# A two-block transformer kernel on one core: first loads, norms at layer boundaries, and the order of gates and compression in the second block

## The chip, the core and the metric

The kernel runs on one core of one Trainium2 chip. The metric is the device time of one execution in microseconds (us); lower is better. A core has a matrix engine (TensorE, PE in the profile; its weight loads are PEld), VectorE (DVE), ScalarE (ACT), GpSimd (POOL) and SyncE (SP), which here only issues DMAs. Each engine works through its own instructions in order. Operands lie in SBUF, matrix products land in PSUM (eight banks of 128 x 512 float32).

## What is computed

`reference()` runs two blocks, one behind the other, in float32. Cut to what matters:

```python
def first_block(x, c, ctx, c_ctx, ...):        # x: 256 tokens x 1024, ctx: 256 tokens x 1024
    for l in range(2):
        sh1, sc1, g1, sh2, sc2, g2 = adaln(c, w_mod[l], b_mod[l])     # silu(c) @ w_mod + b_mod, six rows of 1024
        h  = modulate(rms_norm(x, norm1_g[l]), sh1, sc1)              # rms_norm(x) * g * (1 + sc) + sh
        q, k, v, u_pool, a_conv, b_conv = project_inputs(h, w_in[l], ...)
        ... # differential attention over ctx and x, pooling, convolution of a * sigmoid(b)
        x = x + g1 * (mix @ w_out[l])
        x = x + g2 * swiglu(modulate(rms_norm(x, norm2_g[l]), sh2, sc2), w_ffn_in[l], w_ffn_out[l])
        # in layer 0 the same for ctx, with c_ctx; layer 1 leaves ctx as it is
    return x

def hybrid_layer(x, ...):                      # second block
    z = rms_norm_2(x) @ w_in                   # twenty parts
    y_a = forgetting attention with cumsum(log_sigmoid(f))            # "fox"
    y_b = rg_lru(conv(xb)): a = exp(-8 r softplus(-lam)), gates r, i = sigmoid(...)
    y_c = nsa_attention: keys and values compressed by silu(t @ w1) @ w2, then chosen and windowed
    y_d = gelu(u) * spatial gating of gelu(v)
    merged = sum_n sigmoid(mg_n) * ((y_n * silu(gate_n)) @ w_branch_n)
    return x + merged @ w_out
```

## The kernel before

Activations are kept with features on partitions: `xT` is 128 x 8 x 512, eight tiles `k` of 128 features; columns 0 to 255 are the context, 256 to 511 the input. Weights stream from memory in chunks of 128 x 1024 float32 (512 KB). `weights()` (L339) loads one into `wraw` (4 buffers), ScalarE rounds it to float32r (`whi`, 3 buffers), VectorE forms the rest (`wlo`, 3 buffers). Every large product is then three matmuls, `mm3` (L353): hi x hi, hi x lo, lo x hi. Activations are split alike into `hH` and `hL`.

Order. The code is traced in program order; a planner with a simulated timeline then chooses the order on each engine, by readiness and program order. `tc.issue_after(i)` binds that order: what is traced inside is queued behind `i` on the engine of `i`, and on that engine alone; it is an order of issue, not a wait. All weight loads go out on SP's queue.

Stages, and the names that the change touches:

- **First stage.** `xT` is loaded by two DMAs on ScalarE's queue (L298). Squares, `rows_of_rstd` (L470): the reciprocal norm, 16 matmuls with one column (L432), a power on GpSimd (L359), and a product with ones that spreads it over partitions (L447). `modulation(l, group)` (L502) multiplies silu(c) with eight chunks of `w_mod`, four column groups of 32 at a time (L508), copies, transposes (L515) and adds the bias. Shift and scale come in two halves of eight chunks (`MOD_GROUPS`, first two entries); the chunks use `wraw` and `wmod` (2 buffers) in turn. `norm` (L478) makes per k and per half of the tokens: one VectorE product (L490), the ScalarE part with the shift (L492) and the VectorE rest (L493). Then the four tiles of convolution inputs (`ab`), 24 matmuls of 512 columns each: `feats` (L370) runs the first three of them, with the modulation and norm of the second half between their halves.
- **Layer 0 and 1.** `layer_scalars` (L592), attention, then `project_rows` (L864): the last three of eight output rows are done first for one half of the tokens and then for the other, so that the norm of the first half can begin. `after` (L982) starts the norm for the feed-forward part as soon as the last row is there, `after2` (L1018) that of the next layer. `feats` then runs the first products.
- **Second block.** Token products (`toks`), `log_sigmoid` for 16 and for 4 columns (L1217), the compression: 32 float32 products of 128 x 128 weights with 32 columns (L1146), NSA attention with gate products (`jobs`) between the heads, `batch` (L1455) of activations, the fox attention with `lru_gates` (L1343) traced behind its first head, and the branch products.

## Time and profile before

| | before |
|---|---|
| median of 3 runs | 1428.55 us (1427.3 to 1432.38) |
| the profiled execution, its own time | 1427.89 us |
| span of its instructions | 1426.1 us, 1.8 us lie around it |
| PE busy | 1350.7 us (95%) |
| DVE, ACT, POOL busy | 965.0, 615.3, 237.4 us |
| moved from memory | 210.98 MB, 149 GB/s over the span |
| mean granted PE clock | 0.965 of 2.4 GHz |

PE's clock has two levels here, 2.4 and 1.2 GHz; a stretch with a granted clock of 0.59 spent most of its time on the lower. Idle time of an engine counts only where the end of the kernel waits for it, so the stretches in which PE stands or runs at the lower level are what to look at.

### The profile page before, as it was taken

What the parts mean: (1) busy time and instruction counts of PE and PEld (TensorE: products, weight loads), DVE (VectorE), ACT (ScalarE), POOL (GpSimd) and SP (SyncE); (2) the same over time, 40 slices, a digit from 0 to 9 for tenths busy, and PEclk for the clock granted to TensorE, in tenths of its full rate; (3) what the DMA queues carried; (4) which work ended last, traced back from release to release, by engine and by line L of the source; (5) the groups of instructions that cost most, each with busy time, mean ns of one, the idle gap of its engine ahead of it and who ended that gap; (6) DMA issues with size and microseconds to landing.
All of it is one profiled execution on the core that took longest, in us unless ns stands there. A gap on an engine that the chain in (4) does not pass through costs nothing. (4 is left out here: it accounts for less than half of the span.)

```text
span 1426.1 us, 22731 instructions
## 1 busy us (share of the span) xinstructions
PE 1350.7 (95%) x8750; PEld 1185.2 (83%) x8750; DVE 965.0 (68%) x1924; ACT 615.3 (43%) x1094; POOL 237.4 (17%) x274
## 2 busy tenths in 40 slices
PE   4999999899999999999988899999989998999999
PEld 2699657788888888888966899999877887988999
DVE  4599666677766677738966655555776666657565
ACT  3334454433222222235355443444634558546443
POOL 0056530410000000014534300000442002000000
PEclk8999999899999999999989899999988999999999
DMA  8423541335445567623301355554733423434553
GB/s 327 181 88 134 172 153 45 134 121 190 160 148 166 192 219 238 209 85 104 119 30 60 119 170 185 171 196 159 243 127 111 141 94 105 134 106 158 181 187 125
DMA packets 61309, 213.52 MB, mean 150 GB/s; under 512 B 6928, under 2 KB 8080, under 8 KB 60944
## 3 DMA queue, kind: packets, MB, share of 16 engines
q1 hardware_dynamic: 60768, 209.90, 43.8%
q10 hardware_dynamic: 432, 2.16, 0.4%
q8 instruction: 69, 1.13, 0.3%
q14 instruction: 40, 0.33, 0.1%
HBM read 210.98 MB, written 1.05 MB: 149 GB/s over the span
## 5 line engine op out<-in xcount | busy, mean ns | idle before, releaser
L344 ACT CAST whi<-wraw 128x1024 fp32r<-128x1024 f32 (+2 forms) x296 | 304.8, 1033 | 534.4 <-PE ps_mm L355 243.4
L345 DVE TENSOR_TENSOR wlo<-wraw,whi 128x1024 fp32r<-128x1024 f32 (+2 forms) x296 | 359.3, 1216 | 173.8 <-ACT whi L344 171.5
L354 PE MATMUL ps_mm<-hH,whi 128*128 128x256 f32 (+1 forms) x1056 | 345.1, 329 | 11.1 <-ACT hH L492 9.0
L355 PE MATMUL ps_mm<-hL,whi 128*128 128x256 f32 (+1 forms) x1056 | 342.3, 325 | 1.7 <-DVE hL L493 1.7
L356 PE MATMUL ps_mm<-hH,wlo 128*128 128x256 f32 (+1 forms) x1056 | 342.0, 325 | 0.9 <-DVE wlo L345 0.8
L354 PEld LDWEIGHTS ps_mm<-hH,whi 128*128 128x128 f32 x1056 | 204.3, 195 | 32.8 <-ACT hH L492 11.1
L355 PEld LDWEIGHTS ps_mm<-hL,whi 128*128 128x128 f32 x1056 | 204.4, 194 | 18.8 <-DVE hL L493 3.1
L356 PEld LDWEIGHTS ps_mm<-hH,wlo 128*128 128x128 f32 x1056 | 204.2, 194 | 17.1 <-DVE wlo L345 2.0
L354 PE MATMUL ps_mm<-hidH,whi 128*128 128x256 f32 (+1 forms) x683 | 214.8, 317 | 3.0 <-ACT hidH L350 1.7
L355 PE MATMUL ps_mm<-hidL,whi 128*128 128x256 f32 (+1 forms) x683 | 215.2, 316 | 0.6 <-DVE hidL L351 0.6
L356 PE MATMUL ps_mm<-hidH,wlo 128*128 128x256 f32 (+1 forms) x683 | 214.4, 316 | 0.0
L355 PE MATMUL ps_mm<-wlo,hH 128*128 128x256 f32 (+2 forms) x464 | 145.5, 315 | 4.1 <-DVE wlo L345 4.0
L356 PE MATMUL ps_mm<-whi,hL 128*128 128x256 f32 (+2 forms) x464 | 143.3, 311 | 0.0
L354 PE MATMUL ps_mm<-whi,hH 128*128 128x256 f32 (+2 forms) x464 | 141.3, 313 | 2.0 <-ACT tm L642 1.5
L354 PEld LDWEIGHTS ps_mm<-hidH,whi 128*128 128x128 f32 x683 | 129.5, 190 | 12.0 <-ACT hidH L350 1.9
L355 PEld LDWEIGHTS ps_mm<-hidL,whi 128*128 128x128 f32 x683 | 129.6, 190 | 9.5 <-DVE hidL L351 1.2
L356 PEld LDWEIGHTS ps_mm<-hidH,wlo 128*128 128x128 f32 x683 | 129.5, 190 | 8.1
L465 POOL TENSOR_TENSOR squares<-squares,scr 128x256 f32<-128x256 f32 (+1 forms) x28 | 31.6, 1127 | 561.5 <-ACT scr L464 561.0
L575 DVE CUSTOM_DVE_ANT_0 ps_md<-wmod,tm 128x512 f32<-128x512 f32 x160 | 111.5, 697 | 10.8 <-DMA wmod<-in_w_dram 7.9
L359 POOL TENSOR_TENSOR st<-st,mhalf 128x4 f32<-128x4 f32 (+3 forms) x54 | 69.1, 1284 | 201.7 <-DVE st L627 88.6
L843 DVE SCALAR_TENSOR_TENSOR xT<-ps_mm,modv,xT 128x256 f32<-128x256 f32 x116 | 52.5, 479 | 73.4 <-PE ps_mm L356 73.4
L355 PEld LDWEIGHTS ps_mm<-wlo,hH 128*128 128x128 f32 x464 | 89.5, 193 | 11.4 <-DVE wlo L345 7.1
(345 smaller groups left out, 2011.6 us busy)
## 6 DMA issues: line engine op xcount, KB each, us to landing
wraw<-in_w_dram SPq DMA_DIRECT2D x271, 512.0 KB, 3.4
wmod<-in_w_dram SPq DMA_DIRECT2D x85, 512.0 KB, 4.2
wraw<-in_w_dram SPq DMA_DIRECT2D x32, 448.0 KB, 3.2
xT<-in_x_dram ACTq DMA_DIRECT2D x2, 1024.0 KB, 6.9
single<-in_w_dram SPq DMA_DIRECT2D x8, 256.0 KB, 7.6
wraw<-in_w_dram SPq DMA_DIRECT2D x4, 288.0 KB, 3.5
tm<-in_rows_dram SPq DMA_DIRECT2D x4, 256.0 KB, 6.5
out_dram<-scr SPq DMA_DIRECT2D x8, 128.0 KB, 1.7
```

The lines of the kernel that those rows point to most:

```text
L344: act.copy(out=hi[:, :m], in_=t[:, :m])
L345: P["split"] = dve.tensor_tensor(lo[:, :m], t[:, :m], hi[:, :m].bitcast(F32), op=ALU.subtract)
L354: pe.matmul(ps, a[0], b[0], start=start, stop=False)
L355: pe.matmul(ps, a[0], b[1], start=False, stop=False)
L356: P["product"] = pe.matmul(ps, a[1], b[0], start=False, stop=stop)
L359: pool.tensor_tensor(t, t, mhalf[:, :n], op=ALU.pow)
L465: eng.tensor_tensor(squares[:, lo:hi], squares[:, lo:hi], q, op=ALU.add)
L575: dve.tensor_tensor_reduce(bank("md"), t[:, i * 512:i * 512 + 512], crow[2 * j + i], 1.0, 0.0, ALU.mult, ALU.add, sums[j][:, i * KD + d:i ...
L843: dve.scalar_tensor_tensor(xT[:, d, r], ps[:, s * 256 - lo:s * 256 - lo + 256], M(l, which, 1 - s)[:, d:d + 1], xT[:, d, r], op0=ALU.mult, ...
```

## The change

- The input is loaded by four DMAs on SP's queue, ahead of the weights. Scale and shift come in four quarters of two tiles k each (`first_modulation`, chunks with both); the `ab` weights are packed by the same quarters, for all four tiles at once (`abq`). The sixteen modulation chunks use nine `hid` buffers (now 128 x 1024, hi and lo halves of one tile) and the two `wmod`. `first_products` goes quarter by quarter.
- `weights()` can be queued behind given instructions (`P["behind"]`), and with `P["both"]` every second rounding is done by VectorE (from NSA head 6 to fox head 2).
- `project_rows` holds back six rows instead of three for the attention output of layer 0, and takes a `mm` bank for each half row. In layer 0 the norm of the input half is queued behind the first product of the feed-forward part; at the end of layer 0 that of the context behind the first product of layer 1.
- In layer 1 the first three products of the feed-forward part use `xT * scale` without the norm; the result is multiplied by the norm afterwards, and the shift's share comes from one-column float32 products (24 in all).
- `layer_scalars` is queued behind the norm and the first products; the constants' loads behind the last modulation load.
- `log_sigmoid` for 4 columns moves into the feed-forward part of layer 1, that for 16 columns behind the compressed scores. The compression is turned round: `tbs` (32 columns) is the weight, `w1` streams 128 columns, four column groups; a copy and a product with `sum4` add the groups.
- `batch` chains its activations one behind the other, and behind the last exponentials of NSA; `gb` goes before `gd`; `lru_gates` follows at once, its four Tanh ahead of its four Exp.

```diff
+        if l == 0:
+            for q in range(4):
+                cols = np.arange(q * 256, q * 256 + 256)
+                for k in range(0, 8, 2):
+                    rows(("first", q, k), "w_mod", (l,), np.concatenate([D + cols, cols]), k * 128, 2)
+                rows(("abq", q), "w_in", (l,), np.arange(1792, 2304), q * 256, 2)
-    for k in range(0, KD, 4):
-        act.dma_start(out=xT[:, k:k + 4], ...)
+    for k in range(0, KD, 2):
+        dma.dma_start(out=xT[:, k:k + 2], ...)
     def weights(key):
+        behind = P.pop("behind", ())
...
-        act.copy(out=hi[:, :m], in_=t[:, :m])
+            P["count"] += 1
+            if P["both"] and P["count"] % 2:
+                dve.tensor_copy(hi[:, :m], t[:, :m])
+            else:
+                act.copy(out=hi[:, :m], in_=t[:, :m])
+    def first_modulation(q, pools, p):
+        ps = bank(p)
+        for k in range(0, KD, 2):
+            t = raw_chunk(("first", q, k), next(pools))[0]
+            P["first"] = P["load"]
+            for i in range(2):
+                for g in range(4):
+                    o = i * 512 + g * 128
+                    pe.matmul(ps[g * 32:g * 32 + 32, :128], csil[:, k + i, :], t[:, o:o + 128],
+                              start=(k + i == 0), stop=(k + i == KD - 1), tile_position=(0, g * 32))
+            yield
+        cp = P["wk"].tile([128, 256], F32, name="cp")[:, :128]
+        act.copy(out=cp, in_=ps[:, :128])
+        pe.transpose(ps[:, 256:384], cp, ident)
...
+    def first_products(items):
+        pools = iter(("hid",) * 9 + ("wmod",) * 2 + ("hid",) * 5)
+        ps = [bank("mm" if i < 3 else "sc") for i in range(4)]
+        mods = [first_modulation(q, pools, ("md", "sc")[q % 2]) for q in range(4)]
+        for q in range(4):
+            if q:
+                P["behind"] = P["normed"], P["rest"]
+            wH, wL = weights(("abq", q))
+            for _ in mods[q]:
+                pass
+            norm(h, 0, 512, parts(0, 0, scale1, (0, 1)), range(2 * q, 2 * q + 2), row, True)
+            for k in range(2):
+                for (key, _), t in zip(items, ps):
+                    c = slice(key[2] * 128, key[2] * 128 + 128)
+                    mm3(t, (wH[:, k, c], wL[:, k, c]), tuple(x[:, 2 * q + k] for x in h), q + k == 0, q + k == 4)
+                if q < 3:
+                    with tc.issue_after(P["product"].ins):
+                        next(mods[q + 1])
+                        next(mods[q + 1])
+        P["behind"] = P["normed"], P["rest"], P["first"]
...
-        late = d_list[-3:] if lo == 0 and final else ()
+        late = d_list[-(6 if which == 2 else 3):] if lo == 0 and final else ()
...
+        def unnormed_feat(key, evac):
+            wH, wL = weights(key)
+            t = P["raw"]
+            ps = bank("mm")
+            for k in range(KD):
+                mm3(ps[:, :256], (wH[:, k], wL[:, k]), (h[0][:, k, 0:256], h[1][:, k, 0:256]), k == 0, k == KD - 1)
+            for k in range(KD):
+                pe.matmul(ps[:, 256:257], t[:, k * 128:k * 128 + 128], shift2[:, k:k + 1], start=k == 0,
+                          stop=k == KD - 1)
+            if later:
+                with tc.issue_after(P["product"].ins):
+                    later.pop()()
...
-                feats(items[:3], h, [(0, 256), (256, 512)])
+                feats(items[:3], h, [(0, 256), (256, 512)], then=later.pop())
...
-            for j in range(4):
-                jj = q * 4 + j
-                pe.matmul(ph[:, :32], t[:, j * 128:j * 128 + 128], tbs[p][:, jj * 32:jj * 32 + 32],
-                          start=(jj == 0), stop=(jj == 15))
+            for j in range(4):
+                o = (q * 4 + j) * 32
+                pe.matmul(ph[j * 32:j * 32 + 32, i * 128:i * 128 + 128], tbs[p][:, o:o + 32],
+                          w1[p, q][:, j * 128:j * 128 + 128], start=(q == 0), stop=(q == 3), tile_position=(0, j * 32))
...
-        with tc.issue_after(then.ins):
-            for f, t, kw in items:
-                behind[0] = act.activation(t, t, f, **kw)
+            for f, out, t, kw in items:
+                with tc.issue_after(behind[0].ins) if behind[0] else nullcontext():
+                    behind[0] = act.activation(out, t, f, **kw)
...
+    lru_gates()
```

## Rows read from the trace of the kernel before

**Rows 1.** The page: its span, and PE's busy time, share and instructions.
```profile
span 1426.1 us, 22731 instructions
PE 1350.7 (95%) x8750; PEld 1185.2 (83%) x8750; DVE 965.0 (68%) x1924; ACT 615.3 (43%) x1094; POOL 237.4 (17%) x274
```

**Rows 2.** Windows: stretch, its length, busy time by engine, PEclk, DMA share, GB/s.
```profile
0.00:66.00 66.00, 45.08 (x249) 27.80 (x250) 28.69 (x64) 23.77 (x41) 3.97 (x16) 0.90 0.70 265
...
268.90:285.50 16.60, 12.45 (x58) 10.99 (x57) 11.70 (x22) 5.97 (x13) 8.67 (x10) 0.59 0.20 63
645.40:654.10 8.70, 5.47 (x25) 5.47 (x26) 7.56 (x17) 5.07 (x12) 6.56 (x6) 0.61 0.38 123
805.70:818.00 12.30, 6.28 (x26) 5.49 (x26) 6.39 (x14) 4.46 (x10) 4.96 (x6) 0.58 0.25 87
1010.00:1054.40 44.40, 38.82 (x184) 30.65 (x182) 37.03 (x95) 28.13 (x48) 28.05 (x31) 1.00 0.60 211
1054.40:1070.50 16.10, 16.10 (x76) 15.00 (x77) 6.91 (x12) 0.84 (x5) 3.08 (x2) 0.58 0.30 98
1174.00:1204.00 30.00, 25.37 (x173) 22.43 (x172) 18.11 (x35) 29.16 (x47) 6.98 (x6) 0.89 0.29 98
```

**Rows 3.** Windows of the first stage, ten microseconds each; the last columns are the DMA's.
```profile
0.00:10.00 10.00, 0.28 (x4) 0.23 (x8) 2.08 (x3) 3.85 (x7) 0.86 (x9) 1.00 0.82 312
10.00:20.00 10.00, 9.09 (x65) 5.37 (x58) 2.93 (x5) 1.98 (x4) 1.02 (x1) 1.00 0.95 377
20.00:30.00 10.00, 3.37 (x29) 1.17 (x27) 5.29 (x14) 5.32 (x9) 0.00 (x0) 0.80 0.98 359
...
50.00:60.00 10.00, 9.63 (x35) 7.47 (x35) 3.10 (x8) 1.57 (x3) 0.00 (x0) 0.83 0.01 2
```

**Rows 4.** Timeline of the first stage: start, us, engine, line, what, [idle before <-releaser].
```profile
9.72 1.08 PE L508 MATMUL ps_sc<-wraw,csil 128*32 128x256 f32 x8 [9.72 <-DMA wraw<-in_w_dram]
9.79 1.67 ACT L464 ACTIVATE scr<-xT 128x512 f32<-128x512 f32 x3 [1.70 <-DMA xT<-in_x_dram]
...
20.74 0.59 ACT L475 COPY scr<-ps_aux 128x512 f32<-128x512 f32 x1 [8.76 <-PE ps_aux L447]
...
42.83 0.64 PE L508 MATMUL ps_sc<-wraw,csil 128*32 128x256 f32 x8
...
45.48 0.16 DVE L601 TENSOR_TENSOR lam<-st 128x1 f32<-128x1 f32 x1 [3.08 <-ACT st L599]
...
47.69 0.73 PE L354 MATMUL ps_mm<-hH,whi 128*128 128x512 f32 x2 [0.48 <-ACT hH L492]
...
55.03 0.39 PE L354 MATMUL ps_mm<-hH,whi 128*128 128x512 f32 x1
55.26 0.39 PE L355 MATMUL ps_sc<-hL,whi 128*128 128x512 f32 x1
```

**Rows 5.** Timeline of PE at three layer boundaries: the longest wait of each.
```profile
270.69 0.38 PE L432 MATMUL ps_aux<-ones,squares 128*128 128x1 f32 x2 [1.40 <-POOL squares L465]
...
648.63 0.59 PE L432 MATMUL ps_aux<-ones,squares 128*128 128x1 f32 x2 [3.27 <-POOL squares L465]
...
808.57 0.58 PE L432 MATMUL ps_aux<-ones,squares 128*128 128x1 f32 x2 [2.86 <-POOL squares L465]
```

**Rows 6.** Timeline of PE: float32 products with one column at the upper clock.
```profile
639.92 0.36 PE L432 MATMUL ps_aux<-ones,squares 128*128 128x1 f32 x2
640.14 0.36 PE L432 MATMUL ps_aux<-ones,scr 128*128 128x1 f32 x2
```

**Rows 7.** Groups of PE from 1053 to 1072: count, busy us, mean ns, idle before.
```profile
L1146 PE MATMUL ps_aux<-tm,single 128*128 128x32 f32 x64 | 11.5, 357 | 1.5 <-issue 1.5
```

**Rows 8.** Groups of DVE from 1015 to 1054: count, busy us, mean ns, idle before.
```profile
L1229 DVE TENSOR_SCALAR ls<-ls 128x16 f32<-128x16 f32 (+1 forms) x14 | 3.7, 262 | 0.2
L1228 DVE TENSOR_TENSOR ls<-ls 128x16 f32<-128x16 f32 (+1 forms) x14 | 3.0, 213 | 0.2
```

**Rows 9.** Waits of PE from 1010 to 1056: us in total, times, longest.
```profile
PE ps_mm L355 <- DVE wlo L345: 4.0, 6, 1.0
```

**Rows 10.** Groups of ACT from 1170 to 1204: count, busy us, mean ns.
```profile
L1458 ACT ACT_TABLE_LOAD x7 | 9.0, 1283 | 0.1
```

More of the change, by code (lines that the diff above doesn't have):

```diff
@@ L339, in weights @@
     def weights(key):
-        t, kt, n = raw_chunk(key)
+        behind = P.pop("behind", ())
+        with ExitStack() as order:
+            for i in behind:
+                order.enter_context(tc.issue_after(i.ins))
+            t, kt, n = raw_chunk(key)
+        P["raw"] = t
         hi = whi.tile([128, CHUNK], F32R, name="whi")
@@ L883, in project_rows @@
         ws = {d: make(d) for d in late}
-        banks = {d: bank("mm" if i < 2 else "sc") for i, d in enumerate(late)}
         for s in (first_half, 1 - first_half):
@@ L902, in tile_two_blocks @@
         if not last:
-            queue.extend(modulation(0, g) for g in range(2, 5))
+            queue.extend(modulation(0, g) for g in range(3))
         mix = {}
@@ L1012, in tile_two_blocks @@
                 rows_step(0)
+                if last and f == 10:
+                    decay()
             final = t == 2
@@ L1571, in late_gates @@
         gv = {n: xT[:, o:o + 4, 0:256] for n, o in (("ga", 0), ("gc", 4))}
[L1572 removed]
+        batch(same(AF.Sqrt, [xc[jp] for jp in range(2)]) + same(AF.Silu, [gv[n] for n in ("gc", "ga")]), last_sig)
         lru_scan()
```

255 lines of the change are left out of this document (155 added, 100 removed).

## The prediction

> **What bounds the kernel now.** I read the page first: PE is busy for 1350.7 of 1426.1 us [rows 1], so only 75.4 us of idle can go, and beyond them only work that PE does at its lower level. A windows view of each stage the change touches comes next: it gives PE's idle time (length less busy time) and the granted clock [rows 2]. A mean clock m between the levels 1 and 0.5 means a share 2(1 - m) at the lower level; had that work run at the upper level it would have taken half, so a stretch can return at most idle + busy x (1 - m). The wait that stands ahead of PE at each place then comes from the timelines [rows 5], waits [rows 9] and groups [rows 7, 8, 10]. The profiled execution took 1427.89 us, 0.66 below the median; the sum is made on it.
>
> The first stage differs from the rest. In 0 to 66 us PE idles 20.9 us [rows 2], and the DMA share is 0.95 and 0.98 from 10 to 30 us and almost nothing from 50 [rows 3]: its first half waits for bytes, its second runs through PE's products.
>
> **A. First stage, -5 us (-21 to +10).** Needed are 2.1 MB of input and 20 chunks of 0.524 MB, 12.6 MB. Windows give 3.1, 3.8 and 3.6 MB by 30 us [rows 3]; the other 2.1 MB at the last rate land at 36 us. The input ahead of the weights, 2.1 MB at 312 GB/s, is there at about 7.5 to 8 us instead of 9.8, when the squares begin [rows 4]; the spread norm thus comes near 18.7 instead of 20.7 [rows 4], two tiles of norm follow, first product near 20. The first quarter's weights (4 + 1 chunks, 4.8 MB in all) are there by 15 us and do not hold it. What the input passes on SP are the first weights, about 6 us later than now; PE used them for modulation that nothing was waiting for before the norm.
> Per quarter PE then has 24 products at a cadence of 0.23 us, 5.5 us [rows 4], and four modulation chunks: 0.64 us each now for 256 columns [rows 4], the same number of multiplied values after, 2.6 us. In the code the last two chunks of a quarter stand behind all products of the one before, so copy, transpose, bias and norm lie open three times. Before, one such gap was 43.47 (end of the chunk at 42.83) to 47.69, 4.2 us, partly filled; some 1.2 of it VectorE stood for `lam` of `layer_scalars`, whose releaser is ScalarE [rows 4]. That is now queued behind norm and products, so 3 us remain. It delays nothing: its scalars are first used in attention, behind further products. End: 20 + 5.5 + 3 x (5.5 + 2.6 + 3.0) = 58.8, and 3 more for work at the lower level behind the gaps: 62 against 66. With constants' loads out of the way of weights I take -5. Bounds: by bytes alone the end is 36 + 0.6 + 3 + 5.5 = 45 (-21); with half of the remaining work at the lower level, 76 (+10).
> A page speaks on the move to SP: the Trainium skill, "DMA: Bandwidth & Descriptors", section "Issuing engines are not separate DMA queues", says that DMAs from any engine share the same 16 DMA engines and that several issuers save only issue time; the shares of 0.95 and 0.98 agree.
>
> **B. Layer 0, feed-forward entry, -6 (-9 to -2).** At most 4.15 + 12.45 x 0.41 = 9.3 us [rows 2]. Six late rows instead of three put twelve products each for the input half behind the context's last row, and the squares of POOL that PE waited for [rows 5] then belong to work already covered: 6 rows x 12 x about half of 0.23 = 8 us against a chain of about 7. The input's norm moves behind the first product of the feed-forward part; queued behind it on ScalarE, VectorE and POOL are only roundings of the next weights. I keep 3 us as lost: six rows' weights hold the three `whi`/`wlo` pairs until the second half is done, so the next weights are rounded late.
>
> **C. Layer 0 to 1, -2.5 (-5 to +1).** At most 3.2 + 5.47 x 0.39 = 5.3 [rows 2], behind a wait of 3.27 on squares [rows 5]. The context's norm now goes behind the first product; the input's norm stays open. About half.
>
> **D. Layer 1, feed-forward entry, -2.5 (-6 to +2).** At most 6.0 + 6.28 x 0.42 = 8.6 [rows 2]. The first products no longer wait for the norm, only for one VectorE product and its split. Against that stand 24 one-column float32 products at 0.22 us [rows 6], 5.3 us on PE. Net -3.3; 0.8 is taken off because the close of the first tiles waits for the norm and keeps their `mm` banks.
>
> **E. Start of the second block, -8.5 (-13 to -3).** The compression takes 11.5 us [rows 7] in a stretch with no idle and a clock of 0.58 [rows 2]. After: 8 groups of four products with 128 columns. A group of four with 256 columns takes 0.64 at the upper level [rows 4]; half of it to all of it gives 2.6 to 5.1, at the lower level up to twice. I take 5, and 1.5 for the copy and the product with `sum4`, which now stand in the chain: 11.5 - 6.5 = -5, and -1 for the shorter stay at the lower level.
> The page that bears on this is the Trainium skill, "TensorEngine Tiling (Array Packing)", section "Performance Considerations": with a free dimension of 32 it advises to swap the stationary and the streamed side and use four column tiles, up to 4 times faster. By it 11.5 would become 2.9, and the sum 2.1 us lower; the row of L508 lies between.
> `log_sigmoid` takes VectorE 3.7 + 3.0 us in its 14 steps here, both lengths together [rows 8]; PE waits 4.0 us for `wlo` from VectorE in the same stretch [rows 9], of 5.6 idle [rows 2]. Take -2.5. The steps for 16 columns move behind the compressed scores; what they give is needed only by the fox attention, some 100 us later. Those for 4 columns move beside products of layer 1's feed-forward part; their cost there is two table loads of 1.28 us on ScalarE [rows 10], engines with slack, so 0 to +1; I take +0.5. If ScalarE's roundings were late there it would be the full 2.6.
>
> **F. `batch`, gates, roundings, -2.5 (-7 to +4).** In 1174 to 1204 ScalarE works 29.16 of 30 us, PE idles 4.6 and loses 25.37 x 0.11 = 2.8 to the clock [rows 2]; at most 7.4. Seven table loads of 1.283 stand on the line of `batch` alone [rows 10]; chained in order it needs three, and the chained Tanh and Exp one each at most: some 5 us of ScalarE go. `both` takes half of the roundings from ScalarE here and puts them on VectorE. Behind the longer chain on ScalarE wait the fox exponentials; PE has eight gate jobs beside them. The chain ends with products of `gd`, which the planner can't pull forward, so I take a third.
>
> **How the numbers follow.** -5 - 6 - 2.5 - 2.5 - 8.5 + 0.5 - 2.5 = -26.5: 1427.89 - 26.5 = 1401.4, and with the 0.66 to the median **1402 us**. If every term of this case moves by a third, its own range is 1393 to 1411.
>
> **Rivals.**
> 1. *The three boundaries give nothing (B, C, D at 0).* The products that are put beside the norms need weights; their roundings stand on the same ScalarE and VectorE as the norm, and the buffers are held by the late rows. For it: at all three places ScalarE and VectorE work more than half of the time [rows 2]. Against it: the releaser of the longest wait is POOL's squares each time [rows 5], not weights. 1402 + 11 = 1413. Chance 0.15.
> 2. *The first stage follows the bytes.* If the gaps between quarters are filled by the modulation chunks that arrive meanwhile, the end is 45 instead of 61: 1402 - 16 = 1386. Against it: the order in the code puts two chunks behind the products. Chance 0.08.
> 3. *The first stage and `batch` do not do what they say.* The spread norm comes no earlier, since its chain (squares, one-column products, power, spread) fills 9.8 to 20.7 whatever the loads do, and the planner had a similar order of activations already: A and F at 0, 1402 + 7.5 = 1409.5. Chance 0.11.
> 4. *The other side: the quarters' modulation costs by instruction.* One quarter's four chunks are 64 instructions with 128 columns. The nearest 64 small float32 instructions, the compression, took 11.5 us at the lower level [rows 7]. With products at the lower level too (24 x 0.46 = 11) a quarter takes 11 + 11.5 + 3 = 25.5 instead of 11.1, and the stage ends at 20 + 11 + 3 x 25.5 = 107, 41 later than before: 1402 + 46 = 1448. The whole change becomes slower than no change when the stage ends 21.5 us later than before, that is from a quarter of (87.5 - 31) / 3 = 18.8 us. Against it: four column groups are worked on together in the 0.64 of L508 [rows 4], and the clock was 0.83 from 50 to 60 us [rows 3]. Chance 0.05.
>
> The forecast has the remaining 0.61. 0.5%, 7 us, is about what a measurement of this kernel can tell from no change: faster means below 1421.4, slower above 1435.7. Forecast and rivals 1 to 3 lie below 1421; rivals 1 and 3 together (1420.5) touch the edge, and with small terms they pass it. Faster 0.90, same 0.06, slower 0.04. The range, 1384 to 1418, leaves out rival 4, rivals 1 and 3 together, and tails of the forecast's terms, together under 0.2.
>
> **What would show it.** A: last product of `ab` near 62 us; three gaps of about 3 us between quarters; modulation groups at 0.3 to 0.4 us per four products. If instead they take over 1 us, rival 4 holds. B to D: no PE wait on POOL squares near 270, 640 and 795 us; if waits on `whi` or `wlo` of equal length stand there, rival 1 holds. E: the line of the compression at some 5 us instead of 11.5; waits of PE on `wlo` in the token products halved; granted clock there still below 0.7. F: table loads on the line of `batch` behind NSA down from seven to three, and idle of PE there below 3 us. Wrong would be the whole if an added wait shows up elsewhere: on ScalarE's roundings in the fox attention, where `both` ends at head 2, or on `hid` buffers that first loads and the feed-forward part share.

## The result, and where the time went

The changed kernel takes 1439.06 us (median), before 1428.55: the ratio is 1.0060, with a 95% interval of 1.0032 to 1.0087. It is slower by some 8.6 us; 1402 had been forecast, with a range up to 1418. Its profiled execution has a span of 1440.3 us. The page of the changed kernel shows 9.3 us more busy time of PE (part of it is the same work at the lower clock) and 4.9 us more idle than [rows 1]:

```profile
span 1440.3 us, 23208 instructions
PE 1360.0 (94%) x8966; PEld 1197.7 (83%) x8966; DVE 973.3 (68%) x1954; ACT 608.4 (42%) x1098; POOL 239.2 (17%) x277
```

Windows of the changed kernel, with the columns of [rows 2]: the first stage, the last part of layer 0's attention, the feed-forward entry of layer 0, the step from layer 0 to 1, the feed-forward entry of layer 1, the token products of the second block, the compression, and the stretch behind NSA:

```profile
0.00:66.00 66.00, 43.66 (x383) 32.57 (x384) 31.66 (x88) 25.42 (x44) 5.97 (x16) 0.95 0.72 274
200.00:240.00 40.00, 36.09 (x161) 23.62 (x162) 19.54 (x50) 17.29 (x47) 2.51 (x2) 0.66 0.18 58
277.00:305.00 28.00, 22.58 (x155) 21.22 (x155) 18.22 (x34) 11.85 (x26) 12.54 (x13) 0.87 0.20 69
659.00:689.00 30.00, 20.61 (x130) 18.87 (x129) 20.68 (x45) 16.56 (x29) 12.01 (x13) 0.77 0.29 89
833.00:859.00 26.00, 24.31 (x155) 23.73 (x154) 17.00 (x37) 10.12 (x20) 6.24 (x7) 0.74 0.39 122
1041.70:1085.00 43.30, 39.93 (x243) 32.42 (x245) 35.09 (x74) 26.82 (x45) 27.10 (x31) 1.00 0.63 215
1085.00:1094.00 9.00, 8.18 (x51) 6.06 (x41) 6.65 (x12) 3.95 (x10) 3.08 (x2) 1.00 0.69 229
1188.00:1218.00 30.00, 30.00 (x221) 26.83 (x221) 22.10 (x45) 19.27 (x38) 8.36 (x6) 1.00 0.35 115
```

Two things stand out. In the second block PE idles less and the clock is 1.00 where it was 0.58 and 0.89 [rows 2]. In the first block the clock is low in places, and the step from layer 0 to 1 idles 9.4 us of 30. To see how late the changed kernel is at each point, the same instruction is looked up in both traces (residual sums on VectorE, the gate activations of the feed-forward parts on ScalarE, the first exponential of NSA):

| point | before | changed | late by |
|---|---|---|---|
| first token products of layer 0 | 65.9 | 65.1 | -0.8 |
| first residual sum of layer 0 | 225.7 | 238.3 | 12.5 |
| fourth gate tile of layer 0 | 312.6 | 327.3 | 14.7 |
| last gate tile of layer 0 | 600.4 | 615.1 | 14.7 |
| first scores of layer 1 | 714.1 | 736.2 | 22.1 |
| residual sums of layer 1 (after attention) | 793.5 | 817.4 | 23.9 |
| tenth gate tile of layer 1 | 860.9 | 892.6 | 31.7 |
| last gate tile of layer 1 | 984.7 | 1016.4 | 31.7 |
| first exponential of NSA | 1117.4 | 1131.8 | 14.4 |
| end of the span | 1426.1 | 1440.3 | 14.2 |

So in this pair of executions the first block lost 31.7 us at four places where 16 had been forecast to go, and the second block gave 17.5 back where 10.5 had been forecast. The pair lies 14.2 us apart, the medians' ratio gives 8.6, so single rows of the table overstate; by whole runs the four places cost 26.6 us together and the second block gives 18.0 (e5, below).

### The profile page after: what moved, and what is told of

The parts are those of the page before. It is cut to its first block, busy times and chain, and to the rows that moved or that the text cites. A ratio compares the mean times of both kernels' runs of the same rounds, so it can differ in the third digit from the quotient of the medians.

```text
span 1440.3 us, 23208 instructions
## 1 busy us (share of the span) xinstructions
PE 1360.0 (94%) x8966; PEld 1197.7 (83%) x8966; DVE 973.3 (68%) x1954; ACT 608.4 (42%) x1098; POOL 239.2 (17%) x277
## 4 chain that ended last, share of the span: by engine, by line
PE 84%; DVE 6%; DMA 4%; ACT 2%; POOL 2%; issue 1%; SPq 0%; ACTq 0%; POOLq 0%; DVEq 0%
PE ps_mm L372 22%; PE ps_mm L371 22%; PE ps_mm L373 22%; PE ps_sc L371 2%; DVE wlo L362 2%; PE ps_aux L371 2%; PE ps_aux L373 2%; PE ps_aux L372 2%; PE ps_aux L753 1%; DMA wraw<-in_w_dram 1%; PE ps_sc L372 1%; PE ps_sc L373 1%; DVE cacc L852 1%; PE ps_md L544 1%; PE ps_aux L1546 1%
## 5 line engine op out<-in xcount | busy, mean ns | idle before, releaser
L361 ACT CAST whi<-wraw 128x1024 fp32r<-128x1024 f32 (+2 forms) x292 | 300.5, 1033 | 523.4 <-PE ps_mm L372 268.2
L371 PE MATMUL ps_mm<-hid,whi 128*128 128x256 f32 (+1 forms) x717 | 223.5, 314 | 3.0 <-ACT hid L367 1.7
L372 PE MATMUL ps_mm<-hid,whi 128*128 128x256 f32 (+1 forms) x717 | 223.0, 312 | 0.0
L373 PE MATMUL ps_mm<-hid,wlo 128*128 128x256 f32 (+1 forms) x717 | 222.0, 311 | 0.0
L371 PEld LDWEIGHTS ps_mm<-hid,whi 128*128 128x128 f32 x717 | 136.0, 190 | 11.8 <-ACT hid L367 1.9
L372 PEld LDWEIGHTS ps_mm<-hid,whi 128*128 128x128 f32 x717 | 136.5, 190 | 8.4 <-issue 0.5
L373 PEld LDWEIGHTS ps_mm<-hid,wlo 128*128 128x128 f32 x717 | 136.1, 190 | 7.6
L376 POOL TENSOR_TENSOR st<-st,mhalf 128x4 f32<-128x4 f32 (+3 forms) x54 | 65.2, 1213 | 188.4 <-DVE st L764 61.6
## 6 DMA issues: line engine op xcount, KB each, us to landing
raw<-in_w_dram SPq DMA_DIRECT2D x14, 512.0 KB, 10.2
```

The lines of the kernel that those rows point to most:

```text
L361: act.copy(out=hi[:, :m], in_=t[:, :m])
L371: pe.matmul(ps, a[0], b[0], start=start, stop=False)
L372: pe.matmul(ps, a[0], b[1], start=False, stop=False)
L373: P["product"] = pe.matmul(ps, a[1], b[0], start=False, stop=stop)
L376: pool.tensor_tensor(t, t, mhalf[:, :n], op=ALU.pow)
```

## How the runs are compared

Executions of one kernel lie up to 19 us apart, since stretches at the lower clock fall differently each time; the medians and ratios below are over 3 to 12 executions, each against the kernel before on the same chip. Two more columns help to read them. "Work" is the mean of time x mean granted clock, roughly what the kernel would need at the upper level throughout; "lost" is the rest of the mean time. Work is the steadier of the two: the nine executions of the changed kernel scatter by 2.4 us in work and by 3.3 in time. It does not price parts, though, since a wait at the lower level is counted as half a wait: it falls by 8.1 to 8.8 us in e5, e6 and e7 alike, though e5 has the parts of both others. What parts cost is therefore read from the ratios.

| kernel | median us | ratio to before (95%) | work | lost |
|---|---|---|---|---|
| before | 1428.55 | 1 | 1376.6 | 52 |
| changed | 1439.06 | 1.0060 (1.0032 to 1.0087) | 1379.3 | 59 |
| e1, order 0 to 1 undone | 1429.68 | 1.0021 (0.9996 to 1.0046) | 1376.8 | 54 |
| e2, unnormed undone | 1431.34 | 1.0016 (0.9993 to 1.0040) | 1375.4 | 57 |
| e3, six rows and order undone | 1433.53 | 1.0020 (0.9996 to 1.0044) | 1378.0 | 54 |
| e4, first stage undone | 1430.42 | 1.0018 (0.9994 to 1.0042) | 1376.3 | 55 |
| e5, second block alone | 1411.96 | 0.9874 (0.9849 to 0.9900) | 1367.8 | 44 |
| e6, part E alone | 1417.96 | 0.9896 (0.9861 to 0.9931) | 1368.2 | 48 |
| e7, part F alone | 1422.83 | 0.9968 (0.9942 to 0.9994) | 1368.5 | 56 |
| e8, one-column probe | 1463.63 | 1.0239 (1.0206 to 1.0272) | 1395.9 | 68 |
| e9, last quarter by tile | 1437.82 | 1.0070 (1.0046 to 1.0095) | 1379.2 | 60 |
| e10, shift left out | 1431.45 | 1.0017 (0.9991 to 1.0042) | 1377.0 | 55 |
| e11, order of B undone | 1436.05 | 1.0054 (1.0026 to 1.0082) | 1377.3 | 60 |
| e12, first tiles forced | 1433.28 | 1.0031 (0.9999 to 1.0063) | 1373.2 | 63 |
| e13, VectorE loaded | 1432.72 | 1.0014 (0.9991 to 1.0038) | 1379.4 | 54 |

A difference of two ratios is uncertain by some 0.004, 5 us. One part undone gives 0.0039 to 0.0044, 5.6 to 6.3 us, so each of these four alone stands just at that edge; all four undone together (e5) give 0.0186, 26.6 us, which is far beyond it and about the sum of the four (23.6).

## Experiments

**One part undone at a time.** Theory 1 says that each place has its own cost; its rival says that the clock wanders and no place is to blame.

```diff
e1                       if a:
-                            run()
-                        else:
-                            context_norm.append(run)
+                        run()
```

> The changed kernel with one edit undone: at the end of layer 0 the context's norm runs at once, not behind the first product of layer 1. Theory 1 (the queue moves the stall): in the changed kernel the first products of layer 1 use up all that the input half allows, and the context's norm starts only behind them, so PE waits 4.2 and 2.2 us near 679 with a low clock behind it. Undone, these waits go and the boundary is back to one wait of about 3 us: 7 us less, 1432 against 1439. Rival (the clock wanders): the losses of the changed kernel are low-clock stretches that fall here or there; the total stays within 3 us of 1439.

Measured: 5.6 us less than the changed kernel, for one edit of three lines. What it undoes stands in the changed kernel's timelines of PE and of VectorE (start, us, engine, line, what, idle before and its releaser):

```profile
662.85 0.96 PE L371 MATMUL ps_mm<-hH,whi 128*128 128x256 f32 x3 [2.82 <-ACT hH L502]
673.45 0.38 PE L442 MATMUL ps_aux<-ones,squares 128*128 128x1 f32 x2
679.20 1.19 PE L457 MATMUL ps_aux<-scr,ones 128*128 128x256 f32 x2 [4.24 <-DVE lam L638]
682.55 0.58 PE L371 MATMUL ps_mm<-hH,whi 128*128 128x256 f32 x1 [2.16 <-ACT scr L832]
```

```profile
675.27 0.15 DVE L446 TENSOR_SCALAR st<-ps_aux 128x2 f32<-128x2 f32 x1
677.49 1.23 DVE L362 TENSOR_TENSOR wlo<-wraw,whi 128x1024 fp32r<-128x1024 f32 x1 [0.77 <-ACT whi L361]
678.64 0.42 DVE L453 TENSOR_TENSOR scr<-first,st 128x256 f32<-128x256 f32 x1
```

The planner works on the three first tiles side by side, k by k, so the "first product" behind which the context's norm is queued ends at 673, when the other two have three products left. The one-column products of the norm start there, its VectorE steps stand behind roundings of the next weights, and PE, which has no other work, waits 4.24 us (the step on `lam` that is named ends right behind the `scr` of 678.64 that the product reads). Before, the same steps ran at 648.6, behind the one long wait of that boundary [rows 5]. In e1 one wait on the squares is back and the 4.24 is gone; the second wait, on an activation of ScalarE, was expected to go too and stays (it also stands in e5, with 2.2 us), so it is not the order's. The window of the boundary has 24.48 us of PE work in 30 instead of 20.61. PE in e1:

```profile
659.85 0.59 PE L442 MATMUL ps_aux<-ones,squares 128*128 128x1 f32 x2 [3.28 <-POOL squares L475]
675.11 0.39 PE L371 MATMUL ps_mm<-hH,whi 128*128 128x256 f32 x1 [2.24 <-ACT scr L832]
655.00:685.00 30.00, 24.48 (x164) 23.83 (x163) 25.09 (x50) 17.23 (x30) 13.45 (x13) 0.83 0.33 105
```

The other traces bear it out. From the last gate tile of layer 0 to the first scores of layer 1 the eight with this order take 121.1 to 123.2 us, e1 118.1, and the six with the first block of before (before, e5 to e8, e13) 112.6 to 116.9. So the order is worth some 4 us here; what makes e1 some 3 us longer than those six stays open.

```diff
e2  (after, gate part)
-            if last:
-                unnormed(d)
...
-                if a:
+                if a and not last:
...
-                if t == 0 and last and f < 2:
-                    tiles = [unnormed_feat(*it) for it in items[:2 - f]]
```

> The changed kernel with one edit undone: the feed-forward part of layer 1 starts with the norm, as before, and without the 24 one-column float32 products. Theory 1: the edit took the 6 us of idle away, but its one-column products (5.3 us) brought the clock down to the lower level for 13.7 us while PE was never idle; undone, the boundary costs 6.0 us idle and 10 us of low clock again, 7 us less in all: 1432. Rival: without them the wait on the squares comes back at full length and the low clock behind it too, so nothing is won: 1437 to 1441.

Measured: 6.3 us less, as theory 1 has it. The changed kernel's PE timeline there:

```profile
841.02 1.84 PE L1092 MATMUL ps_mm<-modv,wraw 128*128 128x1 f32 x16
844.00 3.40 PE L1092 MATMUL ps_mm<-modv,wraw 128*128 128x1 f32 x16
848.27 2.13 PE L1092 MATMUL ps_mm<-modv,wraw 128*128 128x1 f32 x10
851.25 1.28 PE L1092 MATMUL ps_mm<-modv,wraw 128*128 128x1 f32 x6
853.70 0.55 PE L371 MATMUL ps_mm<-hH,whi 128*128 128x256 f32 x1 [1.17 <-DVE st L1101]
```

Sixteen instructions (eight products) took 1.84 us at first and 3.40 from 844 on, without PE having been idle in between: the clock went to the lower level while it worked. The 24 products took 8.7 us instead of 5.3, and the products behind them ran at half speed to 857.4. From the eighth residual sum to the tenth gate tile of layer 1 the traces with these products take 103.5 to 106.3 us, e2 101.0, e10 (below) 100.6, and those with the first block of before 100.9 to 101.3: some 5 us.

```diff
e10 (the changed kernel)
-            for k in range(KD):
-                pe.matmul(ps[:, 256:257], t[:, k * 128:k * 128 + 128], shift2[:, k:k + 1], start=k == 0,
-                          stop=k == KD - 1)
...
-                dve.tensor_copy(b, ps[:, 256:257])
+                dve.memset(b, 0.0)
```

> The changed kernel without the 24 one-column products that bring the shift's share in the first tiles of layer 1's feed-forward part; that share is left out and a zero stands in its place. Theory D (small products bring the clock down): the 5.3 us of the products go and the clock stays at 1.0 from 840 to 860, another 3 to 7: 8 to 12 us less than the changed kernel, 1427 to 1430, and better than undoing the whole edit (1432). Rival (the clock falls there because the boundary is thin in any case): the clock falls all the same and only about 5 goes: 1433.

Measured: 6.1 us less, between the two theories, and no better than undoing the whole edit. Without the small products the clock still falls once, and PE waits on the norm again:

```profile
845.39 0.67 PE L457 MATMUL ps_aux<-scr,ones 128*128 128x256 f32 x2 [1.79 <-DVE scr L453]
849.17 0.55 PE L371 MATMUL ps_mm<-hH,whi 128*128 128x256 f32 x1 [3.12 <-DVE scr L1099]
835.00:861.00 26.00, 19.98 (x144) 19.12 (x144) 18.02 (x36) 12.50 (x24) 7.84 (x6) 0.87 0.29 94
```

So most of the idle that the edit removed was filled by its own one-column products: PE idles 6.0 us here, as before [rows 2], and 1.7 with them. Three tiles without the norm do not cover its chain, since their close needs the spread norm. The products cost their 8.7 us and the lower clock behind them, and give back 4.3 of idle.

```diff
e3 and e11 (e11 keeps the six rows)
-        late = d_list[-(6 if which == 2 else 3):] if lo == 0 and final else ()
+        late = d_list[-3:] if lo == 0 and final else ()
...
-                if a:
+                if a and last:
                     later.append(run)
...
-                    feats(items[:3], h, [(0, 256), (256, 512)], then=later.pop())
+                    feats(items[:3], h, [(0, 256), (256, 512)])
```

> The changed kernel with one edit undone: three late rows instead of six at the entry of layer 0's feed-forward part, and the input's norm not behind the first product. Theory 1: that boundary lost 3.3 us against before (waits 0.43, 2.44, 0.95 and 1.57 on the norm, two of 0.5 on weights, instead of 1.40, 0.91, 1.84), so undoing gives 3 us: 1436. Rival: six rows did cover the context's norm, and the loss is the clock's alone; then undoing gives nothing or costs up to 3: 1438 to 1442.

> The changed kernel with six late rows, but the input's norm in layer 0's feed-forward part runs at once and not behind the first product. Theory B (the order is the loss, as at the end of layer 0): the three first tiles are worked on side by side, so the last product of the first of them is nearly the last of all three, and the norm behind it lies open (one-column products at 297, first product of the input's half at 302.9, 1.57 us of waiting and low clock from 304.5). Undone the boundary costs no more than before: 4 to 6 us less than 1438. Rival (the six rows, with their halves of 256 columns and weights held longer, are the loss): 1437 or more.

Measured: 5.7 us less with both undone, 0.9 with the order alone undone. With an uncertainty of 5 us the 0.9 decides nothing between theory B, which wanted 4 to 6, and its rival; and e11's profiled execution was slow elsewhere, with 41 us at the lower level in layer 0's attention. The stretch itself, from the first residual sum to the fourth gate tile of layer 0, says more: 98.0 to 100.4 us in the seven other traces with six rows and the order, 96.5 in e11, 92.6 in e3, and 92.8 to 97.3 in the six with neither. By these single traces the order costs some 3 us and the six rows 1 to 4; six rows alone were not undone. PE waits 6.5 us there in the changed kernel, 5.1 in e11, 2.5 in e3 and 4.4 before. The changed kernel's waits, but for 0.43 us on squares, are on the context's norm, on the input's (the 1.57, which is gone in e11) and on late weights:

```profile
287.32 0.69 PE L371 MATMUL ps_mm<-hH,whi 128*128 128x256 f32 x2 [2.44 <-ACT hH L502]
289.17 0.58 PE L372 MATMUL ps_mm<-hL,whi 128*128 128x256 f32 x1 [0.95 <-DVE hL L503]
302.85 0.50 PE L371 MATMUL ps_mm<-hH,whi 128*128 128x256 f32 x2 [1.57 <-ACT hH L502]
314.05 0.50 PE L371 MATMUL ps_mm<-hH,whi 128*128 128x512 f32 x1 [0.54 <-ACT whi L361]
315.31 0.50 PE L373 MATMUL ps_mm<-hH,wlo 128*128 128x512 f32 x1 [0.53 <-DVE wlo L362]
```

In e3, with three rows, the waits on the context's norm are these two:

```profile
277.38 0.70 PE L457 MATMUL ps_aux<-scr,ones 128*128 128x256 f32 x2 [0.32 <-DVE scr L453]
280.27 0.80 PE L371 MATMUL ps_mm<-hH,whi 128*128 128x256 f32 x2 [2.19 <-ACT hH L502]
```

Six rows leave the first wait for the norm as long as three do. The reason stands on both engines in the changed kernel: VectorE has the norm's operand ready at 281.5, but on PE the product that spreads it is issued behind products of the late rows, at 283.94, and three products later PE has nothing left:

```profile
281.06 0.42 DVE L453 TENSOR_TENSOR scr<-first,st 128x256 f32<-128x256 f32 x1 [0.39 <-POOL st L376]
283.94 0.59 PE L457 MATMUL ps_aux<-scr,ones 128*128 128x256 f32 x2
```

So the late rows cover the norm up to that product and delay it, and most of what comes behind it (VectorE's products and the splits, until 287.32) lies open. What the rest of the difference is made of was not separated.

**The first stage.** e4 puts the two halves of before back (input on ScalarE's queue, chunks of 256 columns, `first_norm`) and leaves all else of the change.

```diff
e4
-    for k in range(0, KD, 2):
-        dma.dma_start(out=xT[:, k:k + 2], ...)
+    for k in range(0, KD, 4):
+        act.dma_start(out=xT[:, k:k + 4], ...)
...
-            first_products(items)
-            items = []
+            feats(items[:3], h, [(0, 512)], first_norm(1))
+            items = items[3:]
```

> The changed kernel with the first stage of before (two halves, input on ScalarE's queue, scale and shift by 256 columns). The stage itself ended 0.8 us earlier in the changed kernel (65.1 against 65.9), but layer 0's attention then lost 12 us, most of it in a low-clock stretch of 27 us from 209 to 236 behind two waits on modulation chunks. Theory 1a: the loss in attention belongs to the new first stage, which shifts the modulation chunks that follow; undone, 11 us less: 1428. Theory 1b: it belongs to that one execution's clock; undone, the total rises by 1: 1440, and the clock from 200 to 236 is 1.0 here or in the other runs of this group that keep the new first stage.

Measured: 6.0 us less, so theory 1a holds in sign, at half of its size (and just at the edge of what can be told); the stretch of 27 us at the lower clock belonged in part to that execution (by the granted clock, the time at the lower level in layer 0's attention is 14 to 41 us in the eight traces with the new stage, 24 in the mean, and 3 to 24, 17 in the mean, in the seven with the old one). Over all traces the place is the same, though, and it is not the stage: the first token products of layer 0 start at 65.1 to 66.4 us in seven traces with the new stage (68.9 in e12) and at 64.0 to 66.0 in the six with the old one and the usual load on VectorE, but the first residual sum comes at 232.1 to 242.4, 236.2 in the mean (229.7 in e12), against 225.0 to 232.7, 228.6 in the mean. The stage itself and the loss behind it, in the changed kernel's PE timeline:

```profile
21.99 0.96 PE L371 MATMUL ps_mm<-hH,whi 128*128 128x512 f32 x3 [1.91 <-ACT hH L502]
32.77 0.97 PE L371 MATMUL ps_mm<-hH,whi 128*128 128x512 f32 x3 [1.91 <-ACT hH L502]
45.19 1.65 PE L371 MATMUL ps_mm<-hH,whi 128*128 128x512 f32 x3 [3.59 <-ACT hH L502]
57.39 0.96 PE L371 MATMUL ps_mm<-hH,whi 128*128 128x512 f32 x3 [1.92 <-ACT hH L502]
153.49 0.41 PE L748 MATMUL ps_aux<-first,e 128*128 128x128 f32 x2 [1.94 <-DVE hid L368]
```

The wait of 3.59 us ahead of the third quarter is longer than the others for a reason of its own. The `log_sigmoid` for 4 columns is traced in layer 1's feed-forward part, but the planner laid it out here, ahead of the modulation's sum on VectorE, although the transpose which that sum reads was done at 41.6:

```profile
43.20 0.16 DVE L960 TENSOR_TENSOR ls<-ls 128x4 f32<-128x4 f32 x1
43.28 0.22 DVE L531 TENSOR_TENSOR modv<-ps_md,colt 128x4 f32<-128x4 f32 x2
```

So these steps did not run beside layer 1; in all eleven traces that have them moved they stand at 40 to 54 us. The wait is 3.6 to 3.8 us in the changed kernel and e11, and 1.96 in the other six traces with the new stage, where that transpose came only when the steps were nearly done (44.4 in e1). The products behind it start no later here (45.19) than in e1 (46.68), so no cost of it can be seen.

The wait at 153 to 155, on a split by VectorE, stands at 1.9 to 2.2 us in seven traces (the changed kernel, e1, e2, e3, e9, e10, e11), with low clock right behind it in all but one, and in none of the six that have the old first stage and the usual load on VectorE. VectorE is full from 66 to 140 us (before: 73.97 of 74.00), with 60 convolution steps of 0.74 us on the `ab` tiles and two first taps on another line. In the new stage the first pair of tiles is gated at 64.2 and the second at 65.4, before at 61.4 and 67.4; the expectations below put this too large. Its steps (count, duration min/median/max in ns, first and last start in us), changed and before:

```profile
L852 DVE SCALAR_TENSOR_TENSOR cacc<-cu,colt,cacc x60: 733/741/1225, 66.0 to 141.5; 128x512 f32<-128x512 f32 x60
```

```profile
L815 DVE SCALAR_TENSOR_TENSOR cacc<-cu,colt,cacc x60: 733/742/1228, 65.1 to 139.0; 128x512 f32<-128x512 f32 x60
```

Three runs ask whether this lateness is the cause.

```diff
e9                    the last quarter's products, in program order
-            for k in range(2):
-                for (key, _), t in zip(items, ps):
+            pairs = [(k, i) for i in range(4) for k in range(2)]      # q == 3
e12                   the same, and each tile bound behind the one before
+                with tc.issue_after(P["product"].ins) if q == 3 and n and k == 0 else nullcontext():
e13                   the kernel before, tap (1, 0) of layer 0
+                    for _ in range(5):
+                        dve.scalar_tensor_tensor(dv, u[:, j, :n, i:i + 256], colt[:, o + i:o + i + 1], av, ...)
```

> The changed kernel with the last quarter's 24 products in another order: one ab tile behind the other instead of all four side by side. Theory A (VectorE's queue): with the new first stage all four ab tiles are done at 64 to 66 us, where before two were done at 57 to 61; VectorE's 62 convolution steps start about 4 us later and end at 142 instead of 137, with VectorE full from start to end, and PE then waits 2.1 us at 154 for a split, with low clock behind it. Done tile by tile the first tile is out some 3 us earlier, the last step ends near 139 and the wait at 154 shrinks below 1 us: 2 to 4 us less than 1438. Rival (the attention's loss is the order of the modulation chunks): the wait at 154 and the total stay, 1437 to 1440.

> As in the run before on the last quarter, but with the order bound: each ab tile's products are queued behind those of the tile before, so that the first pair of tiles is done after 12 of the 24 products. In the run with the order only written down the tiles were still worked on side by side and finished at 63.9 to 65.3 as in the changed kernel, so that run said nothing. Theory A (VectorE's queue): the first pair is out some 2.5 us earlier, the 62 convolution steps end at 139 instead of 141.5, the wait of 2.1 us at 154 shrinks to below 1, and the total goes down by 2 to 4: 1434 to 1436. Rival (order of the modulation chunks, or the clock): steps end earlier, but the total stays at 1438.

> The kernel before with five convolution steps of 0.79 us done twice, into a buffer that nobody reads, in the stretch of layer 0 (66 to 140) in which VectorE is full: 3.9 us more on VectorE and nothing on PE. Theory A (VectorE's queue sets when attention can go on): PE waits at about 154 as in the changed kernel and low clock follows: 4 to 8 us more than before, 1433 to 1437. Rival (VectorE's lateness is hidden there): the same time as before within 2 us, 1427 to 1431.

e9 says nothing: the planner put the tiles side by side again. e12 is 0.0029 below the changed kernel (4 us, within the uncertainty), and the wait is gone. But not for the reason expected: the convolution steps end at 142.2, no earlier. In its PE timeline eleven large products still stand between 152.3 and 155, where the changed kernel had run out of them at 149. In e13 PE waits 2.36 us at 158 on VectorE, with the clock low behind it. That is the wait of a later softmax than the one at 153, and the planner laid VectorE's order out anew here (the last convolution step starts at 159.3 instead of 139.0). The run costs 2 us by the ratio (-1 to 5): not theory A's 4 to 8, and not to be told from nothing.

```profile
158.40 1.12 PE L711 MATMUL ps_aux<-first,e 128*128 128x128 f32 x4 [2.36 <-DVE e L708]
```

So 3.9 us more on VectorE cost nothing that these runs can show, and theory A is not borne out. The wait goes with the order on PE, which the planner lays out anew when the first stage changes. Between the last modulation products and the softmax's product no large product is left in the seven traces that have the wait, and 8 to 12 are left in the seven that have not (one in e13). That is read from the traces, and not shown by an experiment of its own. From 66 to 240 us PE idles 8.2 us in the mean of those seven traces and 5.3 in the six with the old stage; what else makes up the 6 us, and what brings the clock down there, stays open.

**The second block.** e5 has its parts alone; e6 the compression and the two `log_sigmoid`, e7 the order of activations, gates and roundings.

> The kernel before with the parts of the second block alone: compression turned round, both log_sigmoid moved, batch, gates and roundings on both engines; first stage and the three boundaries as before. Theory 1 (costs by place): the second block gave 17 us in the profiled runs (from 31.7 late at the end of layer 1 to 14.2 late at the end), the other parts cost about 28 together; this kernel comes out at 1411 to 1416, faster than before by 0.9 to 1.2%. Rival (the clock wanders): 10 of the 17 are low clock that the second block happened to be spared in that execution; then about 1421 to 1424.

> Only the compression and the two moved log_sigmoid on the kernel before. The prediction's part E gave 8. Theory 1: 8 or a little more, 1418 to 1421, since the line of the compression goes from 11.5 to about 4 us and the waits on wlo in the token products shrink. Rival: the token products in front hold the place (DMA or roundings), and half of it stays: 1424.

> Only batch, gates and the roundings on both engines, on the kernel before. The prediction gave it 2.5, at most 7.4. Theory 1: 2 to 5 us, 1424 to 1426. Rival (roundings moved to VectorE make VectorE late in the fox attention, and eat it): 1428 or more.

```diff
e5 = the changed kernel less the parts undone in e1 to e4, and with
-        with tc.issue_after(P["normed"].ins), tc.issue_after(P["rest"].ins), tc.issue_after(P["product"].ins):
-            layer_scalars(l)
+        layer_scalars(l)
e6 = e5 less lru_gates behind batch, the chain in batch, gb ahead of gd, and
-        P["both"] = hd >= 6
e7 = e5 with the compression and both log_sigmoid as before
```

Measured: e5 18.0 us faster than before, e6 14.9, e7 4.6; the two sum to 19.5. e5 beats both kernels, as theory 1 has it. e6 came out better than theory 1 had it by ratio (10 to 20 us with the uncertainty), e7 within it (0.9 to 8.3). All three also keep the `mm` bank for each half row and the wider `hid` buffers of the change, so each gain holds a share of these, if they have one. The traces agree on part E: from the last gate tile of layer 1 to the first exponential of NSA the eleven with it take 112.8 to 115.5 us, the four without 129.2 to 133.6. PE's compression in the changed kernel, by groups:

```profile
L1284 PE MATMUL ps_aux<-single,tm 128*32 128x128 f32 x64 | 2.0, 274 | 0.5 <-issue 0.5
L1289 PE MATMUL ps_aux<-cstt,scr 128*128 128x32 f32 x4 | 0.6, 232 | 0.0
```

The beginning of the compression in the kernel before, still at the upper clock:

```profile
1054.40:1056.00 1.60, 1.60 (x15) 1.60 (x15) 1.60 (x3) 0.14 (x1) 0.00 (x0) 1.00 0.00 0
```

ScalarE's table loads from 1184 to 1222 in the changed kernel, on the line of `batch` (which now carries those of the gates too):

```profile
L1584 ACT ACT_TABLE_LOAD x3 | 3.8, 1283 | 0.0
```

**One-column products by themselves.**

```diff
e8 (the kernel before, layer 0, behind feed-forward tiles 5, 12 and 19: n = 8, 24, 48)
+                        for i in range(n):
+                            pe.matmul(pa[:, 0:1], ident, ones[:, 0:1], start=i == 0, stop=i == n - 1)
```

> The kernel before with one-column float32 products put, back to back, into three dense stretches of layer 0's feed-forward part, where PE does not wait: 8 behind tile 5, 24 behind tile 12, 48 behind tile 19; their result is not used. Theory 1 (small products bring the clock down without any idle): the 24 and the 48 are followed by a stretch with a granted clock of 0.5, the 8 perhaps not; the kernel is longer than the 17.6 us that 80 products at 0.22 cost, by 7 to 14 us: 1453 to 1460. Rival (only idle brings it down): the clock stays at 1.0 there, 1446.

Measured: 1463.63, above theory 1's end. The next gate tile is later than before by 1.8 us through the 8, by 10.3 through the 24 and by 18.8 through the 48; at 0.22 us [rows 6] they would be 1.8, 5.3 and 10.6. The windows of the three places, none with any idle of PE by the profile's count (it models where a matmul ends, so short gaps between small products would not show; the second and third begin some 2 us behind the first of the products), and the group:

```profile
350.00:359.00 9.00, 9.00 (x49) 7.76 (x48) 4.29 (x8) 3.19 (x4) 0.00 (x0) 1.00 0.56 171
473.00:484.00 11.00, 11.00 (x46) 10.03 (x46) 2.06 (x4) 0.37 (x1) 0.00 (x0) 0.53 0.21 77
598.00:618.00 20.00, 20.00 (x94) 18.86 (x94) 2.23 (x6) 0.00 (x0) 0.00 (x0) 0.57 0.20 72
```

```profile
L1017 PE MATMUL ps_aux<-ones,first 128*128 128x1 f32 x160 | 26.8, 303 | 0.0
```

In the dense part of the feed-forward, where the clock is otherwise 1.00, a run of small products brings it down with PE busy all the time. Their price is double: twice 0.22 for most of them, and large products at half speed behind them. That explains 31 of the 35 us; the other 4 came later in the kernel, where nothing was changed.

## The prediction, step by step

- **A, -5.** Wrong by its scope. The modulation was cheaper than assumed (1.08 us for two chunks) and the spread norm ran at 17.5, but the first product came at 22, since copy, transpose and the norm's own steps (1.9 us of waiting) stand behind the last chunk. The three gaps between the quarters were 2.7, 4.3 and 2.7 us instead of 3.0 each, the middle one behind the `log_sigmoid`. The stage gave nothing (0.8 in the pair above, none over all traces). The sum then stopped at the end of PE's stage: it never asked what VectorE's full queue and the order of the products behind it would do with tiles that are all done at the end. Undoing the part gives 6.0.
- **B, -6.** The step "six rows cover a chain of about 7" failed. From the last residual sum of the context (277.15) to the first product on its norm (287.32) it is 10.2 us; the cover lasted to 284.9, some 7 of the forecast 8, and held up the norm's own product for 2.5 of them. The wait for the norm stayed (2.44 and 0.95 us). The 3 us kept as lost for late weights were mis-sized: waits on weights are 1.1. Of the input's norm the prediction said that only roundings are queued behind the first product; PE waited 1.57 us for that norm, and by single traces the order cost some 3 us. Undoing both gives 5.7.
- **C, -2.5.** The step "the context's norm goes behind the first product" took it for granted that the products of the second and third tile would cover it. Worked on side by side, they end together, and PE waited 4.24 us. Loss 5.6 by e1.
- **D, -2.5.** The 24 products were priced at the upper level [rows 6] and it was taken that removing idle brings the clock back. They brought it down themselves (e2, e8), and most of the idle they removed was idle that they filled (e10).
- **E, -8 with the log_sigmoid.** Right in direction, 14.9 by e6. The mis-sized term was the compression: 11.5 [rows 7] became 2.0 + 0.6, not 5 + 1.5; most of the 11.5 had been at the lower level, and the compression itself probably brought the clock down. That is inferred from e8: the clock was still 1.00 for some 2 us of it, but PE had idled 1.5 us right before [rows 7]. With the products turned round the clock is 1.00 there instead of 0.58 [rows 2], so the sign "granted clock there still below 0.7" was wrong as well. Before, the first 15 of the 64 instructions took 1.60 us at the upper level (window above); all 64 would have taken some 6.8 at that rate, an estimate. Of the 5.8 times from 11.5 to 2.0 the clock is thus some 1.7 and the turn 3.4. The Trainium skill ("TensorEngine Tiling (Array Packing)", "Theoretical Speedup") gives up to 4 times for a dimension of at most 32, and the 3.4 agrees. By the row of L508 the prediction had 2.6 to 5.1 us, and it took the far end. Waits on `wlo` went from 4.0 [rows 9] to 3.0 us. The `log_sigmoid` for 4 columns did not run beside layer 1's products, where the prediction put it, but in the first stage.
- **F, -2.5.** Right in direction, 4.6 by e7 (0.9 to 8.3). ScalarE works 19.27 us of 30 instead of 29.16 [rows 2], the loads on `batch`'s line went from seven [rows 10] to three, PE is never idle there, and the clock is 1.00.
- **The rivals.** Rival 1 named the right three places, with a gain of zero as its worst; it had no row for a loss. Its reason, that ScalarE and VectorE work more than half of the time at all three, misreads [rows 2]: ScalarE works 0.36, 0.58 and 0.36 of them, VectorE 0.70, 0.87 and 0.52. Rival 4, the one on the slow side, was at the wrong part: the quarters' modulation cost 0.27 us per eight instructions. The signs to look for misled as well: the waits on POOL's squares at the boundaries did go (0.43 us is left at 278, none at the other two), and the time rose all the same.

## What to carry to other kernels

A step that is queued behind "the first product" hides only behind what is left after that product in the order that the planner really lays out; look that order up before counting on cover. Price small products not by their own duration but with the clock that they leave behind, and do not count idle that an edit fills with its own extra work as won. When a part moves the end of one engine's stage, follow the order of the other engines on from there until they have caught up. Where executions differ by more than the edit is worth, look the same stretch up in every trace that has the edit and in every one that has not.

## What the runs showed of the hardware

The granted clock can fall to its lower level without any idle of PE: in e8 with 24 and with 48 one-column products in a row (0.53 and 0.57 in the two windows, 1.00 with 8), in the changed kernel at 844 us among 24 such products, and perhaps in the kernel before, over 2 us into 64 instructions with 32 columns, where PE had idled 1.5 us right before [rows 7]. Eight one-column products took 1.84 us at the upper level and 3.40 at the lower. The Trainium skill ("TensorE: Matmul & The Clock Gate", "HAM oscillation — how this bites in real kernels") names gaps in which PE idles as what brings the clock down; the stretches of e8 and the one at 844 have none by the profile's count, so what the runs measured decides here.
